# Seven products in the down projection's two middle groups, with the sums of the weights' quarters made by adding transfers in memory, and sample states multiplied unsplit in fp32

## The chip, the cores and the metric

One core of a Trainium2 chip runs the kernel; seven of the chip's eight cores are idle. The metric is the device time of one execution in microseconds. The core has five engines with a queue each: PE (TensorE, matrix products; PEld is its weight load), DVE (VectorE), ACT (ScalarE), POOL (GpSimd) and SP (SyncE, which here only issues transfers).

## What is computed

One inference step of one decoder layer in fp32, for a prompt of 512 tokens and 8 samples of 8 tokens (576 token columns in all, held as two halves of 288):

```python
z = rmsnorm(x, g_pre_mix) @ w_in                      # GLA and retention branches, 4 heads each, and gates
# both branches, per head: S_t = diag(a_t) S_{t-1} + k_t^T v_t ;  o_t = q_t S_t
#   prompt from a zero state; each sample from its own cached state (128 x 256)
x = x + rmsnorm((sigmoid(gA) * o_gla + sigmoid(gB) * o_ret) @ w_mix_out, g_post_mix)
x = x + rmsnorm(cross_attn(rmsnorm(x, g_pre_xa), mem_k, mem_v, w_xq, w_xo), g_post_xa)
hf = rmsnorm(x, g_pre_ffn)
x = x + rmsnorm(jnp.square(jax.nn.relu(hf @ w_up)) @ w_down, g_post_ffn)      # 1024 -> 4096 -> 1024
```

The new states of prompt and samples and the prompt's memory keys and values are returned too.

## The kernel before

Features lie on the partitions, tokens in the free dimension. Every fp32 operand of a large product is split into a rounded part and a remainder (`split`: ACT casts to fp32r at L92, DVE subtracts at L93), and a product of 128 x 128 weights with 128 x 288 activations is three matrix instructions (L250 to L252, or L280): high by high, low by high, high by low. Weights come from memory as raw tiles of 128 x 1024 (`wfetch`, L179, on SP's queue; four buffers `wraw`), are split by `wsplit`, and taken in order by `wnext`; the list `plan` holds the order.

The stages in time: memory keys and values and the first norm (to about 66 us); the mixers, eight units of a branch and head (`unit`, L889), each with eight weight tiles of 48 matrix instructions and, woven between them as generators that `tick` advances, `prompt()` and `sample()` (to about 600 us); output projection and cross-attention, with the samples' cached keys and values multiplied in plain fp32, four heads side by side on PE (`quarters`, L1240; to about 790 us); the MLP (to the end).

The MLP goes through its 4096 hidden features in four groups of 1024. Group 0 goes up with 8 products per 2 x 2 block (`project`). Groups 1 to 3 go up with seven products (`sevenfold`, L272: the Winograd form on quarters of weights and tokens; four blocks of two weight tiles each). The sums of the tokens' quarters are made once (`sums_f`); the sums of a block's weight quarters are made by four DVE subtractions of 128 x 512 (`begin`, `minus`, L212). Each product is 12 matrix instructions; some add up in the same PSUM tile (`acc`), and a copy by ACT takes an intermediate sum out of it. All four groups go down with 8 products per block (L729: eight weight tiles, 48 matrix instructions each); `y3` gathers the groups.

In `sample()` four pairs of states are loaded, split by ACT and DVE, and each state is multiplied with the queries by two instructions of 128 x 128 with 128 x 256 (L1083, L1084); a third (L1085) makes the state's update. The queries lie in a block pattern `qb` so that all samples add up in one PSUM tile `so`.

The program's lines are not the order of issue. The framework's planner lays out each engine's queue ahead of time; an engine then works its own queue in that fixed order, and waits at an instruction whose operand is not there.

Of the kernel before, what the change touches and what calls it, by code (L numbers as in the profile page):

```python
# [26 lines left out]


RING, STAY, RAW, SEVEN = 0, 1, 2, 3
# [16 lines left out]
C_MG = C_KD + 4  # L46
C_MR = C_MG + 4
C_SG = C_MR + 16
# [9 lines left out]
def decoder_step(ctx, tc, xT, memT, ktc, vc, s_gla, s_ret, w_in, w_ga, w_a2, w_mix, w_xq, w_xk, w_xv, w_xo,  # L58
                 w_up, w_ups, w_down, vecs, cst, gam, y_out, mk_out, mv_out, sg_p, sr_p, sg_s, sr_s):
# [102 lines left out]
    def seven(w, b0):  # L162
        return [(w[b0 + b][:, kh], SEVEN) for b in range(4) for kh in range(2)]

    plan += whole(w_up) + rest(whole(w_up), 0) + whole(w_down)
    for g in range(1, 4):
        plan += seven(w_ups, 4 * (g - 1))
        plan += whole(w_down, 4 * g) + (rest(whole(w_down, 12), 0) if g == 3 else [])
    raws, ready, staying = [], [], []
    wq = []  # L170
    units = []

    def wfetch():
        if plan and sum(m == SEVEN for _, m in raws) < 2:
            src, mode = plan.pop(0), RING
            if isinstance(src, tuple):
                src, mode = src
            raw = wp.tile([P, 1024], F32, name="wraw", bufs=N_RAW)
            nc.sync.dma_start(out=raw if len(src.shape) == 2 else raw.rearrange("p (k n) -> p k n", n=src.shape[2]), in_=src)  # L179
            raws.append((raw, mode))  # L180

    def wsplit():
        if units:
            units.pop(0)()
        elif raws:
            if raws[0][1] == SEVEN:
                begin()
                return
# [4 lines left out]
            pool = staying[-1] if mode == STAY else wp  # L193
            wh = pool.tile([P, 1024], F32R, name="wh")
            wl = pool.tile([P, 1024], F32R, name="wl")
            split(wh, wl, raw)
            ready.append((wh, wl))

    def halves(w):
        return w.rearrange("p (q n) -> p q n", q=2)  # L200

    def begin():


        while len(raws) < 2:
            wfetch()
        p0, p1 = (raws.pop(0)[0] for _ in range(2))
        t = wp.tile([P, 1024], F32, name="wraw", bufs=N_RAW)
        q0, q1, qt = halves(p0), halves(p1), halves(t)

        def minus(out, a, b):
            nc.vector.tensor_tensor(out=out, in0=a, in1=b, op=ALU.subtract)  # L212

        def ring(raw):
            wh = wp.tile([P, 1024], F32R, name="wh")
            wl = wp.tile([P, 1024], F32R, name="wl")
            split(wh, wl, raw)
            ready.append((wh, wl))

        def own(raw, o, n):  # L220
            w = wq[0][:, o:o + n], wq[0][:, o + n:o + 2 * n]
            split(*w, raw)
            ready.append(w)

        def unit_a():
            ring(p0)
            wfetch()

        units.extend([unit_a, lambda: ring(t), lambda: own(p1, 0, 1024),
                      lambda: minus(q1[:, 0], q1[:, 0], qt[:, 0]), lambda: own(q1[:, 0], 2048, 512)])  # L230
        minus(qt[:, 1], q1[:, 1], q0[:, 1])
        minus(q0[:, 1], q0[:, 1], q0[:, 0])
        minus(qt[:, 0], q1[:, 1], q0[:, 1])
        wfetch()

    def wnext(n=P):

        while sum(len(r) == 2 for r in ready) < 2 and (raws or plan):
            while not units and plan and len(raws) + sum(len(r) == 1 for r in ready) < N_RAW - 1:
                n0 = len(raws)  # L240
                wfetch()
                if len(raws) == n0:
                    break
            if not raws and not units:
                break
            wsplit()
        return [a.rearrange("p (k n) -> p k n", n=n) for a in ready.pop(0)]
# [24 lines left out]
    def sevenfold(x, p1, p5, u2, c11, c22, c12, c21):  # L272
# [11 lines left out]
        def more():  # L284
            if units:
                wsplit()

        while len(ready) < 3:
            wsplit()
        acc, b, c = atile()[:, :NH], otile()[:, :NH], gtile()[:, 0, :NH]  # L290
        wa, wc, wb = (ready.pop(0) for _ in range(3))
        prod(acc, wa, 0, "A11", True)
        p1(acc)
        while units:
            wsplit()
        wd = ready.pop(0)
        prod(c, wa, 1, "S1", True)
        p5(c)
        if raws and raws[0][1] == SEVEN:
            begin()  # L300
        prod(acc, wc, 0, "S2", False)
        wsplit()
# [5 lines left out]
        c22(acc)  # L308
        prod(c, wb, 1, "S4", False)
        c12(c)  # L310
        more()
        prod(acc, wd, 0, "A22", False)
        more()
        c21(acc)
# [155 lines left out]
    def project(ah, al, half, evict, others=None, wait=KT, keep=0, end=None):  # L470
# [6 lines left out]
        for i, b in enumerate(order):  # L477
# [9 lines left out]
            for m in range(2):  # L487
# [14 lines left out]
                tick()  # L502

# [143 lines left out]
    xnp = ctx.enter_context(tc.tile_pool(name="xnp", bufs=2))  # L647
# [4 lines left out]
    def add(out, a, b, op=ALU.add):  # L652
        nc.vector.tensor_tensor(out=out, in0=a, in1=b, op=op)  # L653

    def sums_f():

        for j in range(4):
# [5 lines left out]
            add(c2[:, 1], c2[:, 0], c2[:, 1])  # L663
            add(c2[:, 0], c1[:, 0], c2[:, 0], ALU.subtract)
            add(c1[:, 0], c2[:, 1], c1[:, 0], ALU.subtract)
            add(c1[:, 1], c1[:, 1], c1[:, 0], ALU.subtract)
            yield
            split(fsh[:, 2:4, j], fsl[:, 2:4, j], c2)
            split(fsh[:, 0:2, j], fsl[:, 0:2, j], c1)
            yield  # L670

    FQ = {"A11": (fh, fl, 0), "A12": (fh, fl, 1), "A22": (fh, fl, 3),
          "S2": (fsh, fsl, 0), "S4": (fsh, fsl, 1), "S3": (fsh, fsl, 2), "S1": (fsh, fsl, 3)}

    def xf7(n):
        h, l, q = FQ[n]
        return h[:, q], l[:, q]

    y3 = None
    for g in range(4):  # L680
        hh = acta.tile([P, 4, 4, NH], F32R, name="hh", tag="xh")
        hl = acta.tile([P, 4, 4, NH], F32R, name="hl", tag="xl")

        if g == 0:
            lows = []
            for half in range(2):
# [14 lines left out]
                while lows:  # L701
                    lows.pop(0)()
            y3 = bigb.tile([P, KT, NT], F32, name="y3", tag="res")
            side.append(sums_f())
            wq.append(biga.tile([P, 4608], F32R, name="wq", tag="biga"))
        else:
            for b in range(4):
                c1, c2 = (hp.tile([P, 2, NH], F32, name="hr") for _ in range(2))

                def c22(ps):  # L710
                    add(c2[:, 1], ps, c2[:, 1])
                    nc.scalar.activation(c2[:, 1], c2[:, 1], AF.Relu)

                def c12(ps):
                    add(c1[:, 1], ps, c1[:, 1])
                    nc.scalar.activation(c1, c1, AF.Relu)
                    nc.scalar.activation(c1, c1, AF.Square)
                    split(hh[:, 0:2, b], hl[:, 0:2, b], c1)

                def c21(ps):  # L720
                    nc.scalar.activation(c2[:, 0], ps, AF.Relu)
                    nc.scalar.activation(c2, c2, AF.Square)
                    split(hh[:, 2:4, b], hl[:, 2:4, b], c2)

                sevenfold(xf7, lambda ps: nc.scalar.copy(c1[:, 0], ps), lambda ps: nc.scalar.copy(c2[:, 1], ps),
                          lambda ps: nc.scalar.copy(c1[:, 1], ps), lambda ps: add(c1[:, 0], ps, c1[:, 0]), c22, c12, c21)
        if g < 3:
            for k in range(KT):
                ps = gemm_m(quarters(hh, hl), None)  # L729
                y = h2(y3[:, k, :])  # L730
                if g == 0:
                    nc.scalar.copy(y, ps)
                else:
                    add(y, ps, y)
                tick()
            drain()
# [43 lines left out]
def mixers(tc, env):  # L780
    e = Env(env)
    nc, split, split_p, gtile, atile, gemm_m, mm3, f32, h2, tick, side = (
        e.nc, e.split, e.split_p, e.gtile, e.atile, e.gemm_m, e.mm3, e.f32, e.h2, e.tick, e.side)
# [3 lines left out]
    with ExitStack() as st:  # L787
# [23 lines left out]
        qb = c1.tile([P, 1152], F32R, name="qblk")  # L811
        sp = [c1.tile([96, P], F32R, name=f"spad{g}") for g in range(2)]
        nc.gpsimd.memset(f32(qb), 0.0)
# [9 lines left out]
        def q2(ap):  # L823
            return ap.rearrange("p (a t) -> p a t", a=2)

# [33 lines left out]
        def norm(o, t, ret):  # L859
# [13 lines left out]
            on = u2.tile([P, 256], F32, name="on")  # L873
# [15 lines left out]
        def unit(h, ret, second, finish):  # L889
# [12 lines left out]
            kd = u1.tile([P, 2, 3, 32], F32, name="kd")  # L902
            if ret:
# [9 lines left out]
                nc.vector.tensor_tensor(out=qd[:, 512:], in0=qs, in1=cc(C_QDS, 256)[:, h * 64:(h + 1) * 64], op=ALU.mult)  # L913
                qp, qsd = qd[:, :512], qd[:, 512:]
# [505 lines left out]
```

## Time and profile before

| | |
|---|---|
| time, median of 3 runs | 1208.21 us (1207.52 to 1211.23) |
| the profiled execution | 1208.38 us, of which the span is 1206.7 us |
| busy in the span | PE 97%, PEld 95%, DVE 64%, ACT 49%, POOL 13% |
| transfers | 158.36 MB, 131 GB/s on the mean, all on SP's queue |
| granted TensorE clock | 0.992 of full speed on the mean |

A row of a group gives the line, engine, operation, the tiles written and read, shapes and count, then the busy time, the mean duration of one, and the idle time before them with what ended it. A busy time counts overlapping instructions once; one matrix instruction lasts longer than the distance to the next, since they are pipelined.

### The profile page before, as it was taken

The numbers are of one execution on the slowest core, as the hardware profiler recorded it, in microseconds if no ns is written. First come the engines' busy times: TensorE is split into PE (matmuls) and PEld (weight loads), VectorE is DVE, ScalarE is ACT, GpSimd is POOL, SyncE is SP. The second block draws the span as 40 slices with busy tenths as digits, with TensorE's granted clock in tenths as the row PEclk, the third lists the DMA queues.
The fourth block names the chain that finished last, engine by engine and source line by source line (L and its number), as shares of the span: only waits on it lengthen the run. The fifth ranks groups of instructions, "written<-read, shape, count | busy, mean of one in ns | idle before, by whom it ended". The sixth has DMA issues, their size and how long they took to land.

```text
span 1206.7 us, 22033 instructions
## 1 busy us (share of the span) xinstructions
PE 1176.0 (97%) x8990; PEld 1150.4 (95%) x8990; DVE 773.9 (64%) x1344; ACT 590.9 (49%) x1056; POOL 157.3 (13%) x158
## 2 busy tenths in 40 slices
PE   8999999999999999999999989999999999999995
PEld 8999999999999999999999877989999999999995
DVE  6757667566757675858677535686847457555655
ACT  6624556543545354535555434466436316424652
POOL 1621213122312231221001000000000000000000
PEclk9999999999999999999999989999999999999998
DMA  8753423242424232423744666654322321422542
GB/s 273 261 180 98 127 81 117 88 127 75 123 83 133 87 113 86 127 88 93 229 144 143 224 226 231 209 169 139 106 65 83 115 70 58 136 70 71 186 149 68
DMA packets 65877, 158.36 MB, mean 131 GB/s; under 512 B 5904, under 2 KB 34704, under 8 KB 65648
## 3 DMA queue, kind: packets, MB, share of 16 engines
q1 hardware_dynamic: 65776, 156.95, 40.9%
q8 instruction: 71, 1.16, 0.4%
q14 instruction: 30, 0.25, 0.1%
HBM read 140.68 MB, written 16.25 MB: 130 GB/s over the span
## 4 chain that ended last, share of the span: by engine, by line
PE 87%; DVE 6%; DMA 3%; ACT 3%; issue 1%; POOL 0%; POOLq 0%; DVEq 0%; SPq 0%; ACTq 0%
PE psg L251 23%; PE psg L250 23%; PE psg L252 23%; PE psa L280 4%; PE psg L280 2%; PE psa L250 1%; PE psa L251 1%; PE psa L252 1%; DVE wl L93 1%; PE pso L280 1%; DMA wraw<-in_w_xo 1%; PE pso L1240 1%; ACT wh L92 1%; DMA wraw<-in_w_down 1%; DVE res L525 1%; PE psa L957 1%
## 5 line engine op out<-in xcount | busy, mean ns | idle before, releaser
L250 PE MATMUL psg<-xh,wh 128*128 128x288 f32 x1296 | 387.2, 299 | 3.2 <-ACT wh L92 3.2
L251 PE MATMUL psg<-xh,wl 128*128 128x288 f32 x1296 | 383.9, 296 | 2.3 <-DVE wl L93 2.3
L252 PE MATMUL psg<-xl,wh 128*128 128x288 f32 x1296 | 383.5, 296 | 0.0
L93 DVE TENSOR_TENSOR wl<-wraw,wh 128x1024 fp32r<-128x1024 f32 x197 | 243.2, 1236 | 93.8 <-ACT wh L92 92.7
L92 ACT CAST wh<-wraw 128x1024 fp32r<-128x1024 f32 x197 | 206.7, 1050 | 167.8 <-PE psg L252 104.1
L250 PEld LDWEIGHTS psg<-xh,wh 128*128 128x128 f32 x1296 | 244.9, 189 | 5.5 <-ACT wh L92 4.2
L251 PEld LDWEIGHTS psg<-xh,wl 128*128 128x128 f32 x1296 | 244.9, 189 | 3.2 <-DVE wl L93 3.1
L252 PEld LDWEIGHTS psg<-xl,wh 128*128 128x128 f32 x1296 | 244.8, 189 | 0.1
L250 PE MATMUL psg<-hh,wh 128*128 128x288 f32 x512 | 151.8, 297 | 0.7 <-DVE y L759 0.6
L251 PE MATMUL psg<-hh,wl 128*128 128x288 f32 x512 | 150.8, 295 | 0.3 <-DVE wl L93 0.3
L252 PE MATMUL psg<-hl,wh 128*128 128x288 f32 x512 | 150.8, 295 | 0.0
L250 PEld LDWEIGHTS psg<-hh,wh 128*128 128x128 f32 x512 | 96.1, 188 | 1.6 <-issue 1.1
L251 PEld LDWEIGHTS psg<-hh,wl 128*128 128x128 f32 x512 | 96.1, 188 | 0.6 <-DVE wl L93 0.6
L252 PEld LDWEIGHTS psg<-hl,wh 128*128 128x128 f32 x512 | 96.1, 188 | 0.0
L332 POOL TENSOR_TENSOR rs<-ms,mhalf 96x3 f32<-96x3 f32 (+1 forms) x11 | 11.0, 1000 | 523.3 <-DVE ms L325 523.3
L943 ACT COPY vt<-psg 128x512 f32<-128x512 f32 x16 | 9.4, 588 | 77.7 <-PE psg L252 77.7
L653 DVE TENSOR_TENSOR y<-psg,y 128x576 f32<-128x576 f32 x16 | 12.1, 758 | 50.3 <-PE psg L252 50.3
L872 POOL TENSOR_TENSOR rs<-mv,mhalf 128x1 f32<-128x1 f32 (+1 forms) x40 | 26.9, 672 | 109.2 <-DVE mv L867 61.5
L250 PE MATMUL psg<-bh,wh 128*128 128x288 f32 x128 | 38.4, 300 | 1.1 <-ACT wh L92 1.1
L945 DVE COPY vd<-psg 128x96 f32<-128x96 f32 x32 | 6.7, 251 | 50.6 <-ACT vt L943 50.6
L251 PE MATMUL psg<-fh,wl 128*128 128x288 f32 x128 | 38.1, 298 | 0.9 <-DVE wl L93 0.9
L250 PE MATMUL psg<-fh,wh 128*128 128x288 f32 x128 | 38.3, 300 | 0.2 <-ACT fh L92 0.2
(334 smaller groups left out, 2512.0 us busy)
## 6 DMA issues: line engine op xcount, KB each, us to landing
wraw<-in_w_in SPq DMA_DIRECT2D x64, 512.0 KB, 3.7
wraw<-in_w_down SPq DMA_DIRECT2D x38, 512.0 KB, 3.7
wraw<-in_w_ups SPq DMA_DIRECT2D x24, 512.0 KB, 3.7
wraw<-in_ktc SPq DMA_DIRECT2D x16, 512.0 KB, 4.7
wraw<-in_vc SPq DMA_DIRECT2D x16, 512.0 KB, 5.6
wraw<-in_w_xq SPq DMA_DIRECT2D x14, 512.0 KB, 4.7
wraw<-in_w_xo SPq DMA_DIRECT2D x14, 512.0 KB, 5.3
wraw<-in_w_up SPq DMA_DIRECT2D x14, 512.0 KB, 4.7
```

The costliest lines, as they stand in the source:

```text
L92: nc.scalar.copy(hi, src)
L93: nc.vector.tensor_tensor(out=lo, in0=src, in1=f32(hi), op=ALU.subtract)
L250: nc.tensor.matmul(out, ah, bh, start=first, stop=False)
L251: nc.tensor.matmul(out, al, bh, start=False, stop=False)
L252: nc.tensor.matmul(out, ah, bl, start=False, stop=last)
L280: nc.tensor.matmul(out, s[:, q, k], m[:, k], start=first and k == i == 0, stop=k == 3 and i == 2, skip_group_check=True)
L332: nc.gpsimd.tensor_tensor(out=rs[:t, :n], in0=ms, in1=mhalf[:t, :n], op=ALU.pow)
L525: nc.vector.tensor_tensor(out=res[:, kk, c], in0=y[:, kk], in1=rj, op=ALU.add)
L653: nc.vector.tensor_tensor(out=out, in0=a, in1=b, op=op)
L872: nc.gpsimd.tensor_tensor(out=rs[:t], in0=mv[:t], in1=mhalf[:t, 0:1], op=ALU.pow)
L957: nc.tensor.matmul(sc[:, :P], kf[:, ci], qf[:, ci], start=True, stop=True)
L1240: nc.tensor.matmul(acc[rows, :256], x(h), w[:, h], start=first, stop=last, skip_group_check=True, tile_position=(0, 32 * h))
```

## The change

1. Groups 1 and 2 also go down by `sevenfold`. For it, the hidden features' quarters and their sums are kept split (`ha`, `fh[:, 2]`, `hh`); the sums are made block by block by `pairs`. Group 3 goes up by seven and down by eight products as before, group 0 both by eight.
2. The sums of the weights' quarters (T1, T2, T4) are no longer made by DVE. For each of ten pairs of blocks, eight transfers of 512 KB from memory to memory make them in scratch tensors `t_sev`: four copies on SP's queue, four adding transfers on POOL's. The calls of `sums()` stand in the mixers and the projections. All seven quarters of a block are then loaded (seven transfers of 256 KB).
3. In `sevenfold` the order of products is A11, A12, S1, S2, S3, S4, A22 (before: A11, S1, S2, A12, S3, S4, A22).
4. A sample's state is no longer split: one plain fp32 instruction with 8 weight columns per state, four of them side by side on PE as in L1240. Keys, values and scores of the samples are laid out over 128 partitions (before 96), and the output is normed in two tiles of 128 rows and turned by four transposes (before two of 64).

```diff
+SUMS_AT = ((4, 2), (8, 2), (12, 2), (16, 2), (20, 2), (24, 2), (28, 2), (32, 2), (34, 1), (38, 1))
...
+        for n in range(b0, b0 + 4):
+            g, i = n // 2, n % 2
+            b = [w_sev[q, n] for q in range(4)]
+            t1, t2, t4 = t_sev[g]
+            out += [((b[0], t1[i]), RING), ((b[2], b[3]), RING), ((t2[0, i], t2[1, i]), RING), ((t4[i],), LAST)]
...
+        for n, (dst, src, plus) in zip((0, 0, 1, 1, 3, 4, 6, 7), (
+                (t1, b11, 0), (t2[1], b12, 0), (t1, b12, 1), (t2[1], b22, 1),
+                (t2[0], t1, 0), (t2[0], b22, 1), (t4, t2[0], 0), (t4, b21, 1))):
+            steps.setdefault(at + n * pace, []).append((dst, src, plus))
...
+            if plus:
+                nc.gpsimd.dma_start(out=dst, in_=src, accum_op=ALU.add, max_dma_last_dim=8192)
+            else:
+                nc.sync.dma_start(out=dst, in_=src)
...
         prod(acc, wc, 0, "S2", False)
-        wsplit()
-        u2(acc)
-        prod(b, wb, 0, "A12", True)
-        more()
-        c11(b)
+        nc.scalar.copy(c1[:, 1], acc)
+        wmore()
         prod(acc, wc, 1, "S3", False)
...
+    def pairs(c1, c2, sh, sl):
+
+        add(c2[:, 1], c2[:, 0], c2[:, 1], ALU.subtract)
+        add(c2[:, 0], c1[:, 0], c2[:, 0], ALU.subtract)
+        split(sh[:, 2:4], sl[:, 2:4], c2)
+        add(c1[:, 0], c2[:, 1], c1[:, 0], ALU.subtract)
+        add(c1[:, 1], c1[:, 1], c1[:, 0])
+        split(sh[:, 0:2], sl[:, 0:2], c1)
...
+            sevenfold(xh7, c1, c2, lambda: add(y[0], y[0], c1), lambda: None, done21)
...
-                        nc.tensor.matmul(so[:, :256], lq, s0h[:, j], start=False, stop=False)
-                        nc.tensor.matmul(so[:, :256], lq, s0l[:, j], start=False, stop=b == 7)
...
+                        nc.tensor.matmul(so[32 * j:32 * j + 8, o], qsd[:, b * 8:b * 8 + 8], s0[:, j], start=False, stop=True,
+                                         skip_group_check=True, tile_position=(0, 32 * j))
```

## Rows read from the trace of the kernel before

**Rows 1.** The page: busy us, share of the span, instructions per engine.

```profile
PE 1176.0 (97%) x8990; PEld 1150.4 (95%) x8990; DVE 773.9 (64%) x1344; ACT 590.9 (49%) x1056; POOL 157.3 (13%) x158
```

**Rows 2.** Stretches: start:end, length, busy time per engine (instructions), clock, DMA share, GB/s.

```profile
20.00:66.00 46.00, 44.52 (x362) 43.70 (x362) 34.85 (x47) 28.30 (x46) 21.45 (x18) 1.00 0.77 250
66.00:600.00 534.00, 531.60 (x4092) 527.76 (x4091) 358.17 (x742) 262.03 (x525) 118.48 (x111) 1.00 0.36 112
640.00:790.00 150.00, 142.49 (x1167) 127.34 (x1166) 82.06 (x146) 68.21 (x129) 9.21 (x16) 0.97 0.62 204
...
898.00:950.00 52.00, 51.65 (x384) 51.04 (x383) 32.97 (x44) 32.98 (x56) 0.00 (x0) 1.00 0.35 109
950.00:1000.00 50.00, 50.00 (x379) 50.00 (x378) 22.32 (x25) 10.65 (x13) 0.00 (x0) 1.00 0.21 64
...
15.00:20.00 5.00, 5.00 (x44) 4.97 (x42) 4.09 (x9) 2.38 (x4) 0.70 (x1) 1.00 1.04 419
```

**Rows 3.** Groups by line on PE: the cross-attention's fp32 instructions, the transposes.

```profile
L1240 PE MATMUL pso<-wraw,qx 128*32 128x256 f32 x256 | 18.0, 386 | 0.7 <-DMA wraw<-in_vc 0.7
L1017 PE MATMUL psa<-idn,on 128*128 128x128 f32 x64 | 12.2, 272 | 0.0
```

**Rows 4.** Timeline of PE around 108 us (start us, duration) and at 692 us.

```profile
108.09 0.28 PE L1083 MATMUL pso<-s0h,qblk 128*128 128x256 f32 x1
108.21 0.28 PE L1084 MATMUL pso<-s0l,qblk 128*128 128x256 f32 x1
...
692.57 0.64 PE L1240 MATMUL pso<-wraw,qx 128*32 128x256 f32 x8
```

**Rows 5.** Groups by line: splits and sums on DVE and ACT.

```profile
L93 DVE TENSOR_TENSOR wl<-wraw,wh 128x1024 fp32r<-128x1024 f32 x197 | 243.2, 1236 | 93.8 <-ACT wh L92 92.7
L92 ACT CAST wh<-wraw 128x1024 fp32r<-128x1024 f32 x197 | 206.7, 1050 | 167.8 <-PE psg L252 104.1 <-issue 15.2 <-DMA wraw<-in_w_xq 11.0
L212 DVE TENSOR_TENSOR wraw<-wraw 128x512 f32<-128x512 f32 x48 | 33.2, 691 | 1.4
L93 DVE TENSOR_TENSOR hl<-hr,hh 128x576 fp32r<-128x576 f32 x24 | 17.1, 753 | 11.0 <-ACT hh L92 11.0
L92 ACT CAST hh<-hr 128x576 fp32r<-128x576 f32 x24 | 14.8, 667 | 0.0
L653 DVE TENSOR_TENSOR hr<-psa,hr x12: 456/458/459, 907.6 to 1135.9; 128x288 f32<-128x288 f32 x12
```

**Rows 6.** Timeline around 913.7 us: an ACT copy, and the product that waits for it.

```profile
913.38 0.40 ACT L725 COPY hr<-psa 128x288 f32<-128x288 f32 x1
...
913.65 0.29 PE L280 MATMUL psg<-fsl,wh 128*128 128x288 f32 x1
...
913.83 0.40 PE L280 MATMUL psa<-fsh,wh 128*128 128x288 f32 x1
...
914.06 0.29 PE L280 MATMUL psa<-fsh,wl 128*128 128x288 f32 x1
```

**Rows 7.** Timeline of PE inside one product group at 785 us, and of ACT at 920 us.

```profile
784.97 0.29 PE L251 MATMUL psg<-xh,wl 128*128 128x288 f32 x1
785.28 0.72 PE L341 MATMUL psa<-dg,idn 96*128 96x288 f32 x2
785.62 0.51 PE L252 MATMUL psg<-xl,wh 128*128 128x288 f32 x1
...
920.52 1.05 ACT L92 CAST wq<-wraw 128x1024 fp32r<-128x1024 f32 x1 [0.66 <-PE psg L280]
...
921.47 0.68 ACT L716 ACTIVATE hr<-hr 128x576 f32<-128x576 f32 x1
```

**Rows 8.** Timeline of SP's issues at 48 us, and issues by line (size, median us to landing).

```profile
47.99 0.42 SPq L1071 DMA_DIRECT2D s<-in_s_ret  x1
49.61 0.34 SPq L179 DMA_DIRECT2D wraw<-in_w_in  x1
...
wraw<-in_w_down SPq DMA_DIRECT2D x38, 512.0 KB, 3.7
```

More of the change, by code (lines that the diff above doesn't have):

```diff
@@ L169, in decoder_step, with sums @@
+    clock = [0]
+    def sums():
+        for dst, src, plus in steps.pop(clock[0], ()):
+            if plus:
+                nc.gpsimd.dma_start(out=dst, in_=src, accum_op=ALU.add, max_dma_last_dim=8192)
+            else:
+                nc.sync.dma_start(out=dst, in_=src)
+        clock[0] += 1
     raws, ready, staying = [], [], []
-    wq = []
-    units = []
+    wdp = []
     def wfetch():
-        if plan and sum(m == SEVEN for _, m in raws) < 2:
+        if plan:
             src, mode = plan.pop(0), RING
-            if isinstance(src, tuple):
+            if isinstance(src, tuple) and isinstance(src[1], int):
@@ L192, in wsplit, with wmore @@
                 return
[L193 to L196, printed above, removed]
+            n = 512 if mode == LAST else 1024
+            pool = wdp[0] if mode == LAST else staying[-1] if mode == STAY else wp
+            wh = pool.tile([P, n], F32R, name="wh")
+            wl = pool.tile([P, n], F32R, name="wl")
+            split(wh, wl, raw[:, :n])
             ready.append((wh, wl))
[L199 to L205, printed above, removed]
+    def wmore():
+        while plan and len(raws) < N_RAW - 1:
             wfetch()
[L207 to L234, printed above, removed]
+        wsplit()
     def wnext(n=P):
         while sum(len(r) == 2 for r in ready) < 2 and (raws or plan):
-            while not units and plan and len(raws) + sum(len(r) == 1 for r in ready) < N_RAW - 1:
-                n0 = len(raws)
+            while plan and len(raws) + sum(len(r) == 1 for r in ready) < N_RAW - 1:
                 wfetch()
-                if len(raws) == n0:
-                    break
-            if not raws and not units:
+            if not raws:
                 break
@@ L502, in project @@
                 tick()
+            if i % 2:
+                sums()
     def to(y, g, ss):
@@ L662, in sums_f @@
             yield
[L663 to L666, printed above, removed]
+            pairs(c1, c2, fsh[:, :, j], fsl[:, :, j])
             yield
[L668 to L673, printed above, removed]
+    SQ = {"S2": 0, "S4": 1, "S3": 2, "S1": 3}
     def xf7(n):
-        h, l, q = FQ[n]
-        return h[:, q], l[:, q]
+        return (fsh[:, SQ[n]], fsl[:, SQ[n]]) if n in SQ else tuple(
+            t[:, {"A11": 0, "A12": 1, "A22": 3}[n]] for t in (fh, fl))
     y3 = None
@@ L682, in decoder_step, with xh7 @@
         hl = acta.tile([P, 4, 4, NH], F32R, name="hl", tag="xl")
+        plain = g in (0, 3)
+        ha = None if plain else biga.tile([P, 2, 2, 4, NH], F32R, name="ha", tag="biga")
+        def xh7(n):
+            if n in SQ:
+                return hh[:, SQ[n]], hl[:, SQ[n]]
+            return (fh[:, 2], fl[:, 2]) if n == "A22" else (ha[:, 0, n == "A12"], ha[:, 1, n == "A12"])
         if g == 0:
@@ L702, in decoder_step @@
                     lows.pop(0)()
+            xns.close()
+            wdp.append(ctx.enter_context(tc.tile_pool(name="wdp", bufs=1)))
             y3 = bigb.tile([P, KT, NT], F32, name="y3", tag="res")
             side.append(sums_f())
[L705 to L722, printed above, removed]
-                    split(hh[:, 2:4, b], hl[:, 2:4, b], c2)
-                sevenfold(xf7, lambda ps: nc.scalar.copy(c1[:, 0], ps), lambda ps: nc.scalar.copy(c2[:, 1], ps),
-                          lambda ps: nc.scalar.copy(c1[:, 1], ps), lambda ps: add(c1[:, 0], ps, c1[:, 0]), c22, c12, c21)
@@ L727, in decoder_step @@
[L727 to L732, printed above, removed]
-                else:
-                    add(y, ps, y)
-                tick()
-            drain()
+            for k in range(KT):
+                nc.scalar.copy(h2(y3[:, k, :]), gemm_m(quarters(hh, hl), None))
+                tick()
+                if k % 2:
+                    sums()
@@ new lines, in decoder_step, with relu2, done22, done1 @@
+            drain()
+            continue
+        for b in range(4):
+            c1, c2 = (hp.tile([P, 2, NH], F32, name="hr") for _ in range(2))
+            def relu2(c, ps=None):
+                nc.scalar.activation(c, c if ps is None else ps, AF.Relu)
+                nc.scalar.activation(c, c, AF.Square)
+            def done22():
+                relu2(c2[:, 1])
+                if not plain:
+                    split(fh[:, 2, b], fl[:, 2, b], c2[:, 1])
+            def done1():
+                relu2(c1)
+                split(*((hh[:, 0:2, b], hl[:, 0:2, b]) if plain else (ha[:, 0, :, b], ha[:, 1, :, b])), c1)
+            def done21(ps):
+                relu2(c2[:, 0], ps)
+                if plain:
+                    split(hh[:, 2:4, b], hl[:, 2:4, b], c2)
+                else:
+                    pairs(c1, c2, hh[:, :, b], hl[:, :, b])
+            sevenfold(xf7, c1, c2, done1, done22, done21)
@@ L738, in decoder_step, with done21 @@
+        if plain:
+            break
+        for b in range(4):
+            c1, c2 = (hp.tile([P, 2, NH], F32, name="hr") for _ in range(2))
+            y = [y3[:, 2 * b:2 * b + 2, hc(half)] for half in range(2)]
+            def done21(ps):
+                nc.scalar.copy(c2[:, 0], ps)
+                add(y[1], y[1], c2)
+            sevenfold(xh7, c1, c2, lambda: add(y[0], y[0], c1), lambda: None, done21)
     res2 = fsp.tile([P, KT, NT], F32, name="res2", tag="fsh")
@@ L1097, in sample @@
-                t64 = u2.tile([P, 256], F32, name="t64", bufs=1)
-                nc.scalar.copy(t64[:64], so[64:128, :256])
-                nc.vector.tensor_tensor(out=t64[:64], in0=so[:64, :256], in1=t64[:64], op=ALU.add)
-                on = norm(t64[:64], 64, ret)
+                on = u2.tile([P, 2, 256], F32, name="on2", bufs=1)
+                for g in range(2):
+                    o = slice(g * 256, (g + 1) * 256)
+                    nc.tensor.matmul(so[:, o], sp[g], vst[g], start=g == 0, stop=False, skip_group_check=True)
@@ L1105, in sample @@
-                for m in range(2):
-                    nc.scalar.copy(sv(oT[:, m, :]), h2(ot[:, m * 64:(m + 1) * 64]))
+                    nc.scalar.copy(sv(oT[:, m, :]).rearrange("p g (j t) -> p g j t", t=8), ov[:, m, :, :, 0:8])
                 yield
```

250 lines of the change are left out of this document (133 added, 117 removed).

## The prediction

> **What bounds the kernel now.** I read the page first, then the stretches by stage, then the groups by line, the waits and the timeline inside single products. The reader is to see in the page that PE is busy for 1176.0 of 1206.7 us [rows 1]. The stretches show where the rest lies: in the mixers PE is busy for 531.6 of 534 us, in a stretch of plain down projection for all of 50, in a stretch of sevenfold up projection for 51.65 of 52 [rows 2]. Only the cross-attention stretch (640 to 790 us) leaves 7.5 us open, and the first microseconds and the end some more. DVE and ACT have room on the mean. So an instruction that PE no longer has to run is worth its slot, as long as the other engines and the transfers keep their places under PE; and what is taken off DVE is worth nothing by itself. The sum below is made against the profiled execution (1208.4 us, 1.7 us of it outside the span), which is 0.2 us above the median of the runs. A change of 0.3% (3.6 us) is about what can be told from no change.
>
> **Part 1, seven products in two down groups.** 379 instructions in 50.00 us of unbroken work are 0.132 us each [rows 2]. A down group of eight weight tiles has 8 x 48 = 384 of them, 50.7 us; four blocks of seven products of 12 have 336, 44.3 us. Each group saves 6.3 us, both 12.7 us.
>
> **Part 2, the states in fp32.** Removed are 16 instructions per unit, 128 in all, 0.12 us apart [rows 4]: 15.4 us. Added are two sets of four side by side per unit, 16 sets. The nearest row is the cross-attention's: a set of four shows as eight records and lasts 0.64 us [rows 4], and 32 sets are busy for 18.0 us, 0.56 each [rows 3]. The bounds are 0.48 us (the 0.64 less the 0.16 by which a pipelined instruction outlasts its slot, 0.28 against 0.12) and 0.64. I take 0.56, the mean over the row: 9.0 us, so 6.4 saved (5.2 to 7.7). The output is now turned by four transposes of 128 instead of two of 64. A transpose of 128 costs between 0.12 (slot) and 0.19 us (12.2 over 64 [rows 3]), four 0.5 to 0.8; the two that go are worth some 0.2 to 0.4. I take 0.3 us more per unit, 2.4 in all (1.6 to 4). Net 4.0 us saved (1 to 6). The update L1085, the scores and the other transposes keep their number and their 128 or 256 moving columns. The state's splits that go from DVE and ACT, and the smaller work on masks that changes, lie under PE's 531.6 of 534 us: nothing.
>
> **Part 3, the order in `sevenfold`.** S3 now stands right behind S2 and adds into the same `acc`, which ACT must copy out in between; before, A12 stood there. The trace prices such a wait: a copy ends at 913.78, and the waiting product is back in its rhythm at 913.93 (its second instruction at 914.06 less one slot) [rows 6]. A copy that starts only when S2's last instruction has ended (0.29 us, and 0.04 for the signal) and lasts 0.40 would leave PE without S3 for 0.29 + 0.04 + 0.40 + 0.15 - 0.13 = 0.75 us, in 20 blocks 15 us. I take nothing, because the queues don't hold program order: a matrix instruction of another product stands in the middle of one group at 785.28, and ACT casts a weight at 920.52 ahead of a relu that the program puts first [rows 7]. S4 goes to another PSUM tile and its operands are ready, so six of its twelve instructions can be laid into the gap. The uncovered 15 us are a rival.
>
> **Part 4, DVE and ACT inside a block.** An up block of groups 1 and 2 lasts 84 x 0.132 = 11.1 us on PE. On DVE stand in it three remainders of 1024 (1.24 each) and one of 512 (0.69), three sums from PSUM and four of `pairs` (0.46), one remainder of 288 (0.46) and three of 576 (0.75) [rows 5]: 10.4 us. Before it was 4.4 + 4 x 0.69 + 3 x 0.46 + 2 x 0.75 = 10.1 us, and PE lost 0.35 us in four such blocks. On ACT it is about 10.3 us: four casts 3.75, three copies 1.2, relu and square 3.0, casts of activations 2.4; before about 9.2. Both fit, with less to spare. I take 0.25 us per up block of groups 1 and 2, 2 us in all (0 to 10). In a down block DVE has 4.4 + 1.4 + 1.5 = 7.3 us: no wait.
>
> Where up passes to down there is a new edge: the last quarter of the first operand (A11) comes out of S4's sum by 0.46 + 0.68 + 0.68 + 0.67 + 0.75 = 3.2 us [rows 5, 7]; PE has A22 (1.6 us) and three quarters of A11 (1.2 us) to run in that time. 0.4 us remain, and 2.7 if a weight's split (1.05 + 1.24) stands ahead. I take 1 us at each of two edges. Together +4 us.
>
> **Part 5, the sums in memory.** 80 transfers of 512 KB are added, 42 MB beside 158, and a block's weights come as 1.75 MB in seven issues per 11.1 us (158 GB/s; the trace reaches 419 [rows 2]). A weight tile lands 3.7 us after its issue [rows 8], so a group's six dependent steps need at least 22 us, and the first group has hundreds. In the mixers transfers use 0.36 of the engines' time [rows 2], and 80 x 512 KB at 419 GB/s is 100 us of 534: there they can hide. No row shows a transfer from memory to memory, an adding one, or one on POOL's queue; their bounds are nothing (hidden) and the prices under the rivals. I take nothing, nearest to the 0.36.
>
> The sum: 1208.4 - 12.7 - 4.0 + 4.0 = 1195.7, so **1196 us**.
>
> **Rivals.**
>
> *A, the copies run ahead (the other side).* The first copies wait for nothing and need no buffer in SBUF. SP's queue takes such transfers early: a sample's state that belongs behind the first unit's weights is issued at 47.99, before its first `w_in` tile [rows 8]. If the 20 free copies stand near the front, 10.5 MB at 419 GB/s are 25 us of a time in which 0.77 to 1.04 of the transfer engines is taken [rows 2], and the weight loads queue behind them. Three tiles ahead cover some 9 us. 16 to 25 us lost give 1216. Against it: SP could be filled by its own loads there. It decides the sign from 12.4 us lost.
> The Trainium skill (DMA: Bandwidth & Descriptors, Issuing engines are not separate DMA queues) says that transfers of all issuing engines run on the same 16 DMA engines and interleave, so that POOL's queue would not shield the weights; in this trace SP alone issues, so no run shows it.
>
> *B, the adds hold POOL's and SP's queues.* An adding transfer waits for the one before it at the head of POOL's queue, and behind it stand the norms' powers and the rotary sums on which the mixers' products wait; copies that wait for an add hold the weights on SP in the same way. One landing more than planned is 3.7 us [rows 8]. If 5 of the 40 adds meet work that PE is about to need, 18 us are lost: 1214. For it: the planner has fixed the order, and POOL works 118 us in the mixers [rows 2]. Against: five adds per unit leave room.
> The Trainium skill (SBUF — State Buffer, Who interferes with whom) lets GpSimd's descriptor writing stand still while VectorE runs a copy in a two-port mode. With up to 1.24 us per add, VectorE's longest row here, 40 adds would stand 50 us longer, an estimate from that page; no run here shows a POOL transfer.
>
> *C, S3's wait stays open*, or ACT is late in the fuller blocks: +15 us less the 2 taken, 1209, no change.
>
> *D, the late sums fall on the cross-attention.* Groups 7 to 9 stand in the projections; 24 transfers are 12.6 MB, 30 us of engines busy to 0.62 [rows 2]. If they double its open 7.5 us: 1203.
>
> **How the numbers follow.** Forecast 0.52, A 0.15, B 0.13, C 0.12, D 0.08. Faster than 0.3%: the forecast, D and a little of C, 0.63. Slower: A, half of B and some of C, 0.24. The same: the rest, 0.13. The low end is the sum with the best bounds, 1208.4 - 12.7 - 6 = 1190, and 3 us for waits that may close. The high end goes through A: 1220. The forecast's own range is 1189 to 1202.
>
> **What would show it.** Right: about 44 us per down group of 1 and 2, no wait on `acc` before S3 with S4's instructions in between, state sets of 0.5 to 0.6 us, no idle PE beside the memory-to-memory transfers. Wrong: PE idle in the first 100 us behind weights that land late (A); POOL or SP waiting for transfers with PE waiting for them (B); 0.7 us of idle per block behind the copy of `acc` (C); more waits for `w_xq` and `w_xo` (D).

## The result, and the profile after

The changed kernel takes 1221.91 us (median of four runs, 1220.94 to 1224.05); the kernel before, on the same chip, 1209.72. The ratio is 1.0104 (95% interval 1.0087 to 1.0121): 12 us slower, where 12 us less was forecast. The page of the changed kernel's profiled execution (span 1219.2 us): busy us, share, instructions, then the transfers, the queue of the adding transfers alone (the copies go with all else), and the memory's traffic.

```profile
PE 1170.7 (96%) x8910; PEld 1128.2 (93%) x8910; DVE 756.9 (62%) x1372; ACT 596.1 (49%) x1068; POOL 179.6 (15%) x205
...
DMA packets 84503, 216.06 MB, mean 177 GB/s; under 512 B 8528, under 2 KB 37328, under 8 KB 81072
...
q0 software_dynamic: 3200, 20.97, 9.9%
...
HBM read 198.36 MB, written 58.20 MB: 210 GB/s over the span
```

PE has 5 us less to do than before [rows 1], and yet the span is 12.5 us longer: PE stands idle for 48.5 us instead of 30.7. Where, is found by cutting both executions at the same events, each the first start of a group of matrix instructions on PE's timeline. In the changed kernel the last three cuts are these (start us, duration):

```profile
568.37 0.38 PE L245 MATMUL psg<-bh,wh 128*128 128x288 f32 x1
...
810.44 0.29 PE L245 MATMUL psg<-fh,wh 128*128 128x288 f32 x1
...
868.12 0.29 PE L245 MATMUL psg<-hh,wh 128*128 128x288 f32 x1
```

The table has the length of each stage for every kernel run in this study: the front up to the first `psg<-xh`, the mixers up to the first `psg<-bh`, output projection and cross-attention up to the first `psg<-fh`, group 0's up projection up to the first `psg<-hh`, and the rest. All in us, from the profiled execution.

| kernel | front | mixers | cross | up 0 | rest | span | median of runs |
|---|---|---|---|---|---|---|---|
| before | 61.7 | 509.4 | 220.9 | 56.4 | 358.3 | 1206.7 | 1208 to 1210 |
| after | 62.2 | 506.1 | **242.1** | 57.7 | 351.1 | 1219.2 | 1221.9 |
| no_sums | 61.9 | 504.7 | 221.4 | 56.4 | 350.6 | 1194.9 | 1197.8 |
| state_only | 62.4 | 504.7 | 222.2 | 56.4 | 358.1 | 1203.8 | 1205.4 |
| before_transfers | 62.7 | 534.7 | 247.5 | 57.7 | 359.7 | 1262.3 | 1264.0 |
| sums_pool | **82.2** | 511.7 | 219.9 | 57.9 | 350.5 | 1222.2 | 1223.2 |
| pool_gated | 62.0 | 505.4 | 233.3 | 56.4 | 350.6 | 1207.7 | 1212.3 |
| sums_early | 62.2 | **611.1** | 223.9 | 57.9 | 350.6 | 1305.6 | 1303.9 |
| early_a12 | 62.2 | 609.7 | 221.8 | 56.4 | 345.5 | 1295.5 | 1298.0 |
| sp_early_gated | 62.6 | 620.0 | 220.8 | 57.9 | 345.5 | 1306.8 | 1306.7 |
| pool_early_a12 | 62.7 | 510.6 | 221.4 | 56.4 | 344.6 | 1195.7 | 1202.8 |
| pool_spread_a12 | 62.0 | 536.0 | 217.3 | 56.4 | 344.6 | 1216.2 | 1213.4 |
| pool_split_a12 | 62.1 | 515.8 | 222.9 | 56.4 | 345.1 | 1202.3 | 1206.2 |
| after_a12 | 61.7 | 506.5 | 247.5 | 57.5 | 345.7 | 1218.8 | 1217.8 |

Mixers and rest gain 10.5 us; the cross-attention's stage loses 21.2. The view of that stage (start:end, length, busy per engine, clock, DMA share, GB/s), first in the kernel before, then in the changed kernel, with two of its short pieces, then PE's waits in it (us, times, longest):

```profile
571.10:792.00 220.90, 212.26 (x1686) 196.01 (x1686) 136.18 (x219) 111.26 (x197) 12.19 (x20) 0.98 0.60 195
...
568.30:810.40 242.10, 217.90 (x1687) 196.90 (x1686) 137.27 (x218) 111.53 (x197) 21.91 (x31) 0.98 0.72 227
...
681.00:685.00 4.00, 2.05 (x17) 1.44 (x10) 3.13 (x6) 2.54 (x4) 1.22 (x2) 0.96 1.13 445
...
695.00:700.00 5.00, 1.51 (x24) 0.45 (x16) 0.69 (x1) 0.50 (x1) 0.00 (x0) 1.00 1.00 285
```

```profile
PE psg L245 <- ACT wh L95: 14.4, 11, 4.7
PE psg L246 <- DVE wl L96: 5.3, 9, 1.2
PE pso L1262 <- DMA wraw<-in_vc: 2.0, 1, 2.0
```

Of the 21.2 us, 15.6 are idle time of PE (24.2 us where 8.6 stood before); the rest stands as busy time of as many instructions, and no view here takes it apart. PE waits for weights: for their cast, and the cast waits for the transfer. The longest wait can be followed through the timelines of SP, POOL and ACT (for a transfer the start is its issue):

```profile
676.84 0.80 SPq L212 DMA_DIRECT2D wraw<-in_w_xq  x2
677.69 0.47 SPq L196 DMA_DIRECT2D t_sev<-t_sev  x1
678.21 1.21 SPq L196 DMA_DIRECT2D t_sev<-in_w_sev  x2
681.03 3.02 SPq L212 DMA_DIRECT2D wraw<-in_vc  x3
685.32 0.33 SPq L212 DMA_DIRECT2D wraw<-in_w_xq  x1
...
684.73 0.78 POOL L194 DMA_DIRECT2D t_sev<-in_w_sev  x1 [2.22 <-DMA t_sev<-t_sev]
686.35 0.78 POOL L194 DMA_DIRECT2D t_sev<-in_w_sev  x1 [0.84 <-DMA t_sev<-in_w_sev]
687.60 0.78 POOL L194 DMA_DIRECT2D t_sev<-in_w_sev  x1 [0.47 <-DMA t_sev<-in_w_sev]
...
700.25 1.04 ACT L95 CAST wh<-wraw 128x1024 fp32r<-128x1024 f32 x1 [4.75 <-DMA wraw<-in_w_xq]
```

```profile
DMA to landing us min/median/max: 4.5/7.8/14.9
```

Three copies and three tiles of `in_vc` stand on SP between the tiles of `w_xq`, and three adds are issued by POOL around the last of these tiles. The last line is from the view of the tile `wraw`, of its transfers issued between 676 and 702 us: the median takes 7.8 us to land and the slowest 14.9, as long as from the issue at 685.32 to the cast at 700.25. From 695 to 700 the transfer engines are full and PE runs 1.5 of 5 us. 22 transfers of the sums are issued in this stage, 11 on each queue.

### The profile page after: what moved, and what is told of

It is laid out like the page before. It is cut to its first block, busy times and chain, and to the rows that moved or that the text cites. A ratio compares the mean times of both kernels' runs of the same rounds, so it can differ in the third digit from the quotient of the medians.

```text
span 1219.2 us, 22249 instructions
## 1 busy us (share of the span) xinstructions
PE 1170.7 (96%) x8910; PEld 1128.2 (93%) x8910; DVE 756.9 (62%) x1372; ACT 596.1 (49%) x1068; POOL 179.6 (15%) x205
## 5 line engine op out<-in xcount | busy, mean ns | idle before, releaser
L96 DVE TENSOR_TENSOR wl<-wraw,wh 128x1024 fp32r<-128x1024 f32 x237 | 280.6, 1188 | 126.3 <-ACT wh L95 125.6
L95 ACT CAST wh<-wraw 128x1024 fp32r<-128x1024 f32 x237 | 239.5, 1013 | 138.3 <-PE psg L247 59.4
L245 PE MATMUL psg<-hh,wh 128*128 128x288 f32 x256 | 75.9, 297 | 0.7 <-DVE y L777 0.6
L246 PE MATMUL psg<-hh,wl 128*128 128x288 f32 x256 | 75.5, 295 | 0.3 <-DVE wl L96 0.3
L247 PE MATMUL psg<-hl,wh 128*128 128x288 f32 x256 | 75.3, 295 | 0.0
L245 PEld LDWEIGHTS psg<-hh,wh 128*128 128x128 f32 x256 | 48.1, 188 | 1.3 <-issue 1.1
L246 PEld LDWEIGHTS psg<-hh,wl 128*128 128x128 f32 x256 | 48.1, 188 | 0.6 <-DVE wl L96 0.6
L247 PEld LDWEIGHTS psg<-hl,wh 128*128 128x128 f32 x256 | 48.0, 188 | 0.0
L891 POOL TENSOR_TENSOR rs<-mv,mhalf 128x1 f32<-128x1 f32 x48 | 27.9, 585 | 98.8 <-DVE mv L886 49.6
L246 PE MATMUL psg<-bh,wl 128*128 128x288 f32 x128 | 38.1, 298 | 1.3 <-DVE wl L96 1.3
```

The lines of the kernel that those rows point to most:

```text
L95: nc.scalar.copy(hi, src)
L96: nc.vector.tensor_tensor(out=lo, in0=src, in1=f32(hi), op=ALU.subtract)
L245: nc.tensor.matmul(out, ah, bh, start=first, stop=False)
L246: nc.tensor.matmul(out, al, bh, start=False, stop=False)
L247: nc.tensor.matmul(out, ah, bl, start=False, stop=last)
L891: nc.gpsimd.tensor_tensor(out=rs[:t], in0=mv[:t], in1=mhalf[:t, 0:1], op=ALU.pow)
```

## The experiments

**The transfers left out, and the state part alone.**

```diff
-        for dst, src, plus in steps.pop(clock[0], ()):
+        for dst, src, plus in ():
...
-            t1, t2, t4 = t_sev[g]
+            t1, t2, t4 = w_sev[1, 2 * g:2 * g + 2], w_sev[2:4, 2 * g:2 * g + 2], w_sev[3, 2 * g:2 * g + 2]
```

> The changed kernel without the 80 transfers: nothing is summed, and the seven-product blocks load plain quarters of the weights in the places of the sums (as many transfers of the same size), so the output is not the reference's. It gives what the rest of the change is worth. If the working of parts 1, 2 and 4 holds and the transfers are the whole of the loss: cross stretch 220 to 222 us, mixers 504 to 507, up and down stages as in the changed kernel, about 1200 us (faster by 0.6 to 1.0%). If something else in the change lengthens the cross stretch: above 1212 us.

Measured: 1197.8 us, ratio to before 0.9905 (0.9883 to 0.9926). The loss is all in the transfers: they cost 24 us, of which 20.7 in the cross stage, 1.4 in the mixers, 1.3 in the first up projection. This kernel's trace also tells how far ahead of its use a weight tile is issued, from SP's issue to ACT's cast, matched in order for the tiles that go through `wraw`: a median of 26.1 us for `w_in` (in the mixers), 10.5 for `w_xq` and 6.3 for `w_xo` (in the cross stage). The medians to landing are 3.7, 4.4 and 5.4 us. So the mixers have some 22 us of slack, and the cross stage has 1 to 6. PE's waits for weights in the cross stage, in this kernel:

```profile
PE psg L245 <- ACT wh L95: 3.9, 3, 1.8
PE psg L246 <- DVE wl L96: 2.3, 3, 0.9
```

state_only is the kernel before with `sample()`, `norm` and the masks of the changed kernel:

```diff
-        sp = [c1.tile([96, P], F32R, name=f"spad{g}") for g in range(2)]
+        sp = [c1.tile([P, P], F32R, name=f"spad{g}") for g in range(2)]
...
+                        nc.tensor.matmul(so[32 * j:32 * j + 8, o], qsd[:, b * 8:b * 8 + 8], s0[:, j], start=False, stop=True,
+                                         skip_group_check=True, tile_position=(0, 32 * j))
```

> The kernel before with the samples' states unsplit in fp32 alone (part 2). By the working of the prediction the mixers shrink by 4.0 us (1 to 6) and nothing else changes: about 1205 us. The changed kernel's mixers were 3.3 us shorter with the transfers beside them; if those cost something there, this run gains more than that.

Measured: 1205.4 us, ratio 0.996 (0.9945 to 0.9974), and the mixers 4.7 us shorter: part 2 is worth what was worked out, and a little more. A set of four states lasts 0.62 us, and the next instruction starts 0.55 us after it began:

```profile
108.53 0.62 PE L1079 MATMUL pso<-s,qsd 128*8 128x256 f32 x8
109.08 0.51 PE L1084 MATMUL psa<-vs,ks 128*128 128x256 f32 x2
```

**The transfers earlier, and in the kernel before.**

```diff
-SUMS_AT = ((4, 2), (8, 2), (12, 2), (16, 2), (20, 2), (24, 2), (28, 2), (32, 2), (34, 1), (38, 1))
+SUMS_AT = ((0, 2), (2, 2), (4, 2), (6, 2), (8, 2), (10, 2), (12, 2), (14, 2), (16, 2), (17, 2))
```

> All 80 transfers of the sums are made in the mixers: a new pair of blocks begins every 2 calls instead of every 4 (the last starts at call 17, its last transfer is at call 31). Theory D (the 33 transfers that stand in the projections delay the weights there): the stretch from the first product with bh to the first with fh falls from 242 back to about 221 us, the wait of psg for wh at L95 in it from 13 us to about 3, and the mixers stay PE-bound; about 1201 us, faster than the kernel before by 0.5 to 0.9%. Rival 1 (the longer stretch comes from something else in the change, the layout in SBUF or the planner's order): the stretch stays at 238 to 244 us, 1219 us or more. Rival 2 (the transfers cost wherever they stand): the mixers grow by what the stretch loses, 1212 to 1220 us.

Measured: 1303.9 us, ratio 1.0781 (1.0759 to 1.0803). The cross stage is back at 223.9, as D said, but the mixers lose 105 us, more than any theory had. The transfer engines are not full there: where it is worst, they move nothing. SP's timeline in this kernel, the two stretches inside its gap, and the longest of SP's waits in the mixers:

```profile
220.76 0.33 SPq L212 DMA_DIRECT2D wraw<-in_w_in  x1
221.18 0.39 SPq L1095 DMA_DIRECT2D s<-in_s_gla  x1
221.66 0.49 SPq L196 DMA_DIRECT2D t_sev<-t_sev  x1
259.73 1.18 SPq L1114 DMA_DIRECT2D out_sgs<-sn  x2
260.96 1.14 SPq L196 DMA_DIRECT2D t_sev<-in_w_sev  x2
262.15 0.58 SPq L212 DMA_DIRECT2D wraw<-in_w_in  x1
```

```profile
235.00:245.00 10.00, 7.44 (x57) 6.62 (x55) 7.72 (x23) 5.68 (x17) 4.02 (x6) 1.00 0.29 54
245.00:255.00 10.00, 3.96 (x14) 2.97 (x15) 4.89 (x17) 4.46 (x11) 2.53 (x4) 0.61 0.00 0
```

```profile
SPq L1114 <- DVE sn L1111: 195.3, 10, 47.8
SPq L1114 <- DVE sn L1109: 92.2, 5, 37.4
```

For 38 us SP stands at the store of a sample's new state, and the next weight tile stands behind the store. PE runs out of weights, and runs only the state's own chain, one dependent step after another, until the store can go; its granted clock has a mean of 0.61 there, so it is at the lower of its two levels for most of the time.

```diff
+            if plus:
+                nc.gpsimd.dma_start(out=dst, in_=src, accum_op=ALU.add, max_dma_last_dim=8192)
+            else:
+                nc.sync.dma_start(out=dst, in_=src)
```

> The kernel before, with the 80 transfers alone added at the places that they have in the changed kernel; nothing reads what they make, so the sums are made twice. Theory D: the stretch bh to fh grows from 221 to 238 to 244 us and the rest stays, about 1228 us (slower by 1.5 to 1.9%). Rival 1 (something else in the change): within 4 us of the kernel before. Rival 2 (transfers cost everywhere): the mixers grow as well, over 1235 us.

Measured: 1264.0 us, ratio 1.0461 (1.0429 to 1.0493). The cross stage loses 26.6 us without any other part of the change, so D holds for it. But the mixers lose 25 as well, and the time lies where the second rival had it (over 1235 us). PE's waits in these mixers are not for weights; the longest are for the normed outputs `on` of the heads:

```profile
PE psa L1130 <- DVE on L899: 5.0, 2, 2.9
```

What makes up the 25 us was not taken apart: PE is idle for 18.2 us of these mixers, against 1.3 before.

**Which queue.**

```diff
-                nc.sync.dma_start(out=dst, in_=src)
+                nc.gpsimd.dma_start(out=dst, in_=src, max_dma_last_dim=8192)
```

> The changed kernel with the 40 copies issued on POOL's queue too, so that SP never holds a weight behind a copy that waits for an add; the same bytes at the same calls. If in D it is the order of SP's queue (weights held behind a waiting copy): the stretch bh to fh falls to 221 to 227 us, about 1203 us. If it is the transfer engines (share near 1 in stretches, each weight landing later): the stretch stays at 236 to 244 us, about 1220 us. Rival B (POOL's queue held by waiting transfers) would cost more here than in the changed kernel, in the mixers too.

Measured: 1223.2 us, ratio 1.012 (1.0097 to 1.0144). Neither theory was tested in the cross stage, because the copies ran ahead: on POOL's queue they were laid where the queue was free, from 1.3 us on, the adds with them, and the last transfer was issued at 299 us. The cross stage is back at 219.9, and the front loses 20.5 us. From 20 to 66 us in this kernel, against [rows 2]:

```profile
20.00:66.00 46.00, 32.75 (x231) 31.88 (x232) 25.81 (x38) 20.24 (x31) 13.48 (x17) 0.81 0.99 325
```

That is rival A, which the changed kernel does not show (its front is 62.2 us), on the other queue and at its forecast price of 16 to 25 us.

pool_gated has the copies on POOL's queue too, and gives each free copy something to wait for:

```diff
+            if plus is None:
+                nc.gpsimd.dma_start(out=dst[0, 0:1, 0:1], in_=late)
...
-            sums()
+            sums(kd[0:1, 0, 0, 0, 0:1])
```

> All 80 transfers on POOL's queue, and each of the 20 free copies made to wait for a tile of its call (a 4-byte transfer of that tile into the place that the copy then overwrites), so that they stand at the calls of the changed kernel and not at the front. SP holds no weight behind them, the bytes in the cross stretch are those of the changed kernel. If the loss there is SP's queue held by copies: cross 220 to 226 us, front back at 62, about 1202 us. If it is the share of the 16 engines: cross 236 to 244 us, about 1220 us.

Measured: 1212.3 us, ratio 1.002 (1.0004 to 1.0036). The cross stage takes 233.3 us with 24 transfers of the sums in it (18 from `w_sev`, 6 within `t_sev`). It lies between the two expectations: about 12 us stay, which can be put down to fuller engines, and the other 9 of the 21 go when the copies leave SP's queue.

```profile
567.40:800.70 233.30, 216.53 (x1687) 198.42 (x1686) 136.57 (x220) 111.05 (x197) 31.61 (x50) 0.96 0.75 239
```

The split is an estimate, and holds only as far as the two orders compare; the profiled execution is also 2.9 us below the median of its ten. The stage's transfers on SP's queue are 42.87 MB, as in the kernel before. SP's view of the changed kernel lists no wait at the head of a copy; what the copies take is lead: the `w_mix` tiles are issued a median of 11.5 us ahead of their cast there, 16.8 in pool_gated and 17.0 in no_sums.

pool_early_a12 has this edit, the early schedule, and A12 back between S2 and S3:

```diff
+SUMS_AT = ((0, 2), (2, 2), (4, 2), (6, 2), (8, 2), (10, 2), (12, 2), (14, 2), (16, 2), (17, 2))
...
+        prod(c, wa, 1, "S1", True)
...
+        prod(acc, wc, 0, "S2", False)
+        nc.scalar.copy(c1[:, 1], acc)
+        prod(b, wb, 0, "A12", True)
+        add(c1[:, 0], b, c1[:, 0])
```

> The same with the calls of the early schedule (all transfers in the mixers) and with A12 between S2 and S3. If the 105 us that the early schedule lost in the mixers came from SP's queue (a copy or a late state store at its head with weights behind it): mixers 506 to 514 us, cross 221, rest 345, about 1194 to 1202 us, faster than before by 0.6 to 1.3%. If they came from the engines' share or from the waits of POOL's queue: mixers 540 us or more, over 1225 us.

Measured: 1202.8 us (1197.4 to 1206.7), ratio 0.9935 (0.9909 to 0.9961): faster than both kernels. With the 80 transfers in them, the mixers take 510.6 us in the profiled execution, which is the fastest of the four (1197.4 us). In the two stretches shown, the transfer engines are fuller than in the cross stage of the changed kernel, and PE is idle for next to nothing, though a weight tile of the first stretch landed as late as 11.9 us after its issue (last line, tile `wraw`):

```profile
130.00:200.00 70.00, 69.96 (x546) 68.47 (x545) 42.05 (x94) 38.88 (x75) 28.23 (x40) 1.00 0.91 246
...
340.00:410.00 70.00, 69.88 (x540) 67.94 (x539) 40.14 (x92) 27.66 (x59) 28.21 (x36) 1.00 0.84 226
...
DMA to landing us min/median/max: 3.7/4.5/11.9
```

The transfers are not free there: these mixers take 5.9 us more than those of no_sums. Taking the 5 to 6 us of the order of products (below) off the 1197.8 of no_sums, an estimate, the 80 transfers still cost about 11 us at the median.

sp_early_gated puts the copies of that kernel back on SP, and changes nothing else.

```diff
-                nc.gpsimd.dma_start(out=dst, in_=src, max_dma_last_dim=8192)
+                nc.sync.dma_start(out=dst, in_=src)
```

> The kernel with the early schedule on POOL, the waits on tiles and A12 between S2 and S3 (1202.8 us, mixers 510.6), with one thing changed: the 40 copies are issued on SP's queue again, the adds stay on POOL's. If SP's queue is what lost the 100 us of the early schedule there: mixers 560 to 620 us, 1255 us or more, with SP waiting tens of us at state stores. If it was the place to which the free copies ran ahead: mixers 508 to 516 us, 1200 to 1208 us.

Measured: 1306.7 us, ratio 1.08 (1.0782 to 1.0818), mixers 620.0. The same transfers at the same calls cost 104 us more from SP's queue than from POOL's. SP waits for `sn` at the stores of states again (259 us in 15 waits), and at copies for the small transfers that gate them (58 us in 6):

```profile
SPq L1116 <- DVE sn L1113: 178.4, 10, 38.1
...
SPq L198 <- DMA t_sev<-kd: 48.5, 5, 13.0
```

So the early schedule lost its time in the order of SP's queue and not in the transfer engines. The gates did not help on this queue: early_a12 below, which differs from this kernel in nothing but the gates, takes 1298.0 us, 8.7 less.

**When, on POOL's queue.** Both kernels are pool_early_a12 with another schedule. pool_spread_a12 begins a pair of blocks every three calls; pool_split_a12 has the last two pairs at the end of group 0's up projection and in its down projection.

```diff
+SUMS_AT = ((1, 2), (4, 2), (7, 2), (10, 2), (13, 2), (16, 2), (19, 2), (22, 2), (25, 2), (27, 2))
...
+SUMS_AT = ((1, 2), (5, 2), (8, 2), (12, 2), (15, 2), (19, 2), (22, 2), (26, 2), (47, 0), (49, 0))
```

> As the kernel with all transfers gated on POOL's queue in the mixers and A12 between S2 and S3, but a new pair of blocks begins every 3 calls instead of every 2, so that the transfers fill the whole of the mixers evenly. In the denser schedule the mixers took 510.6 us, without any transfer 504.7. If their 5.9 us come from the density: mixers 506 to 508, about 1199 us median. If every transfer costs the same wherever it stands: 510 us, 1203 us as there. Pairs that begin at call 25 and 27 may reach into the projections: then the cross stretch is a few us over 221.

> The same, with eight pairs in the mixers (every 3.5 calls) and the last two, which are wanted latest, at the end of group 0's up and in its down projection, where the transfers of the kernel before move 65 to 140 GB/s. If what decides is how full the engines are beside the weights: mixers 505 to 507, cross 221 to 223, down of group 0 unchanged at 51, about 1196 to 1199 us, the fastest of all. If a transfer costs PE time wherever weights are loaded beside it: 2 us or more appear in the down projection of group 0, and it is no better than the spread version.

Measured: 1213.4 us (1204.3 to 1219.5), ratio 1.0024 (0.9999 to 1.0048), and 1206.2 us (1201.5 to 1213.0), ratio 0.9985 (0.9968 to 1.0002). Both forecasts of the time missed: thinner was not better (the intervals of both ratios lie above that of pool_early_a12). The profiled execution of pool_spread_a12 is 4.4 us above its median, so its stages in the table are those of a longer execution. Waits of PE and of POOL in the mixers of the spread kernel:

```profile
PE psa L1037 <- DVE on L899: 8.2, 3, 4.9
PE psa L1125 <- DVE on L897: 6.8, 2, 3.8
```

```profile
POOL t_sev L198 <- DMA t_sev<-in_w_sev: 69.6, 17, 7.7
...
POOL t_sev L194 <- ACT vt L962: 31.1, 3, 13.6
```

PE waits for the normed outputs `on`, whose power (`rs`) runs on POOL, and POOL stands at transfers that wait for a tile or for the one before. That is rival B. That one is the cause of the other is argued from the queue's order alone; no run took it apart. Group 0's down projection did carry two pairs at no cost (rest 345.1).

**The order of the products.** The early kernel and the changed kernel with A12 between S2 and S3 (the diff of pool_early_a12's second part):

> As the kernel with early sums, and in sevenfold A12 stands again between S2 and S3 (A11, S1, S2, A12, S3, S4, A22), so that ACT's copy of acc has 1.6 us before S3. If the 4.3 us that the seven-product stretch has over its instructions come from the open end of that wait (3.1 us, 16 times 0.2): 3 to 4 us less than with early sums alone, and the wait on the copy gone. If they come from fuller DVE and ACT: within 1 us of it, or slower, because the weights of S2 are wanted 1.6 us earlier.

> The changed kernel with A12 between S2 and S3, all else as it is. In the pair of early kernels this order took 5.1 us from the stages behind the first down projection and 1.5 from the first up projection. If that holds here: from the first product with hh to the end 345 to 346 us for 351.1, and 1215 to 1217 us for 1221.9, still slower than the kernel before, because the transfers stand where they stood.

Measured: 1298.0 us beside the 1303.9 of sums_early, and 1217.8 us (ratio 1.007, 1.0048 to 1.0091) beside 1221.9. The rest falls from 350.6 to 345.5 and from 351.1 to 345.7 us, and the wait on the copy of `acc` (below), 3.1 us before, is gone in the first of them and 0.4 us in the second. The 1.5 us in the first up projection do not follow the order: it takes 57.5 in after_a12 and 57.9 in sp_early_gated, both with A12 back. That cause is open.

## Why the prediction was wrong

**Part 5 is the step that failed:** "I take nothing, nearest to the 0.36." The transfers cost 24 us. The 0.36 was a mean of the mixers, and there the choice was nearly right (1.4 us). But 22 of the transfers stand in the cross stage, whose share before was 0.60, and there each costs about 1 us. Rival D named the place and was priced far too low: doubling the stage's open time adds 7.5 us, measured were 20.7. What part 5 left out is how far ahead of their use the loads run (rival A has it for the front alone, as some 9 us). In the cross stage weights landed up to 14.9 us after their issue (7.9 before), and a `w_xo` tile is issued only 5.8 us ahead of its cast on the median; in the mixers of pool_early_a12 they landed up to 11.9 us after it, with some 26 us of lead, and PE waited for none. The copies on SP's queue shorten that lead on top: with them gone to POOL's, 9 of the 21 us went.

The Trainium skill (DMA: Bandwidth & Descriptors, Issuing engines are not separate DMA queues) says that transfers from all issuing engines interleave on the same 16 DMA engines. The trace agrees: all on POOL's queue, the transfers still cost some 12 us in the cross stage. But the Trainium skill counts, in the same section, only issue time as saved by another queue, and the runs differ there: with 80 transfers in the mixers, SP's queue cost 104 us more than POOL's.

**Parts 1 and 4** came out right in their sum, not in place. From the first product with `hh` on, the prediction had -12.7 + 4.0 = -8.7 us; no_sums has -7.7 against before. With A12 back it is -13.7 (pool_early_a12), and a down group of seven products takes 44.0 us (44.3 forecast; 45.6 in the changed kernel). So no net loss is left for fuller engines or for the edges between up and down, where part 4 put its 4 us.

**Part 3** was taken as nothing, because S4's instructions would fill the gap. They do in part, as the timeline of the changed kernel shows in one block (start us, duration):

```profile
936.82 0.29 PE L275 MATMUL psa<-fsl,wh 128*128 128x288 f32 x1
936.96 0.30 PE L275 MATMUL psg<-fsh,wh 128*128 128x288 f32 x1
...
937.37 0.40 ACT L295 COPY hr<-psa 128x288 f32<-128x288 f32 x1
937.49 0.29 PE L275 MATMUL psg<-fsh,wl 128*128 128x288 f32 x1
937.62 0.29 PE L275 MATMUL psg<-fsl,wh 128*128 128x288 f32 x1
937.83 0.40 PE L275 MATMUL psa<-fsh,wh 128*128 128x288 f32 x1
938.06 0.29 PE L275 MATMUL psa<-fsh,wl 128*128 128x288 f32 x1
```

```profile
PEld psa L275 <- ACT hr L295: 3.1, 16, 0.2
```

S2 ends, six instructions of S4 follow, and S3 starts when ACT's copy is out, 0.2 us late, 16 times. That wait is 3.1 us in all. The order back is worth 5.1 to 6.0 us in the rest, in three pairs of kernels (351.1 to 345.7 in the changed one): most of rival C's 15 us is covered, not all, and what makes up the other 2 to 3 us is open.

**Part 2** was right: 4.0 forecast, 4.7 measured in the mixers, and a set takes 0.55 us of PE where 0.56 was taken. **Rivals A and B** did not happen in the changed kernel: its front is 62.2 us, and PE has no wait for `on` in its mixers. A came when the copies were moved to POOL's queue (sums_pool). Waits for `on`, B's sign, came in pool_spread_a12, and also with the copies on SP: some 17 us in the mixers of sums_early, some 8 in those of before_transfers. Of the rule on GpSimd's descriptor writing (the Trainium skill, SBUF — State Buffer, Who interferes with whom) the adds show nothing: 40 took 0.78 to 0.98 us each to issue. The 1.24 us of the prediction's estimate was a subtraction's row, not a copy's. Its 158 GB/s for a block's weights should be 165 (seven transfers of 256 KB are 1.84 MB); nothing hung on it.

Parts 1 to 4 alone were worked out at 1195.7 us, since part 5 stood at nothing; without the transfers the kernel takes 1197.8. That the two are so near is partly luck: part 4 had 4 us too much, and part 3 had 5 to 6 too little.

## What to carry to other kernels

Work that only moves bytes is priced at the stage where it falls, by how full the transfers are there and how far ahead the loads run, and not by a mean; and before that, by what its queue carries behind it. A transfer that nobody waits for yet should not stand on the queue that loads what the bound engine needs next. A transfer that depends on nothing may be laid out early. On POOL's queue it helped to give it something to wait for (1223.2 to 1212.3 us); on SP's, where weights stand behind it, the same gate cost 8.7 us.

## What the runs showed of the hardware

In the changed kernel a transfer of 512 KB from memory to memory landed a median 5.7 us after its issue as a copy on SP's queue and 6.9 as an add on POOL's, beside 3.7 for a weight tile before [rows 8]. The share of the 16 engines alone told little: 0.91 over 70 us of the mixers of pool_early_a12 came with 0.04 us of idle PE, and 0.72 over the cross stage of the changed kernel with 24 us (8.6 before, at 0.60). The kernels with all transfers on POOL's queue spread by up to 15 us from run to run, where the kernel before spreads by about 6; why is open.
